# Hybrid attention + PEER layer: group A's keys projected ahead of the transposes of group B's queries, and two pieces of GpSimd work given to VectorE

## The chip, the cores and the metric

One core of a Trainium2 chip runs the whole program. The metric is the device time of one execution in microseconds (us). Engines are named as the profile names them: PE (TensorE, matmuls and transposes), DVE (VectorE), ACT (ScalarE), POOL (GpSimd), SP (SyncE, which issues every transfer here).

## The reference

One decoder layer on 256 tokens of width 1024, in float32. The input is normalised and projected once; the projection is split into group A (sparse attention with compressed, selected and window branches, 8 heads, 2 key/value heads) and group B (latent attention, 8 heads with 96 channels per query and key). Both are mixed by one output projection, and a product-key expert layer (PEER) follows. What the change touches:

```python
proj = rmsnorm(x, norm1_gain) @ w_in                 # q, kc, vc, ks, vs, kw, vw, gate (A), cq, ckv, kr (B)
# group B
q = (rmsnorm(c_q) @ w_uq).reshape(B, S, 8, 96);  kv = (rmsnorm(c_kv) @ w_ukv)
k = concat([k_nope, broadcast(k_rope)]);  q, k = rmsnorm(q, q_gain), rmsnorm(k, k_gain)
q, k = rope(q), rope(k);  p = softmax(q @ k.T * scale, causal);  o_b = p @ v
# group A: k_slc, k_win = rope(rmsnorm(proj columns)); three softmaxes, gated sum -> o_a
h = x + concat([rmsnorm(o_a), rmsnorm(o_b)]) @ w_out
return h + peer_ffn(rmsnorm(h))                      # q projection, top-k, 2 x 128 expert matrices
```

## The kernel before

Tokens stand in two tiles of 128 (`tt` 0 and 1). Every float32 operand of a large product is kept as a rounded part ("hi") and the remainder ("lo"), and a product is three passes: hi·hi, lo·hi, hi·lo. ACT writes the hi part (`split_pack`, L278 for half a pack, L271 for a quarter), DVE or POOL the lo part (DVE at L282, 128x1024; POOL at L273, 128x512).

The input weights come as seven packs, `win[0]` to `win[6]`. Packs 3 and 4 hold group A's queries, pack 5 its keys (ks, kw), pack 6 its values (vs, vw). `mm_pack` (L315) multiplies one token tile by one pack: 24 matmuls. `aq` takes packs 3 and 4, `ak[tt]` takes pack 5 in its first 256 columns and pack 6 in its last 256.

Group B: `b_proj(tt)` multiplies the latents, squares and sums them (L448, L455), takes the power −1/2 on POOL (`rsqrt`: DVE L149, then POOL L150, called the pow below), scales keys `kn` (L458, L459) and queries `qn` (L462), multiplies by the norm weights (keys L460, queries L464) and rotates the queries (L337 to L340). `b_qkT(tt)` (L473) transposes `kn` and `qn`, 8 transposes each, and ACT copies the result (L474). `unit_B` is one group of heads: scores `sB` (L630, L631), row maximum on DVE (L634), exponentials on ACT (L638), scaling on DVE (L640, L642), transposes `pTB` (L648), a copy on ACT (L601), the product with the values `oB` (L656). `finish` (L608 to L618) normalises a group's output and writes its hi and lo parts (`mix`: ACT L610, DVE L611). `a_norm(tt, ...)` (L485 to L494) normalises and rotates group A's queries (8 heads) and later its keys (4 heads); `a_qT` (L506) and `a_kT` (L518) transpose them. `hidden` (L543) and `compress_out` make the compressed keys. `wo_mm` (L999) is the output projection, `unit_A` (L674 to L709) group A's heads.

Up to the line that takes `bp` apart, all engines run in the order of the code. In the stretch that follows, PE and SP are in the order of the code, and DVE, ACT and POOL are put in order by the tile scheduler. From `side = Side(7)` on until `norm2(1)`, SP alone is fixed; PE, DVE, ACT and POOL are in the scheduler's order, which follows the order of the code as a priority and its own estimates of when an instruction is ready. So a line that moves in the code can move many rows on four engines. `beside(gen, n)` emits one pass of a product and then `n` steps of the waiting units (`side`); `do(gen)` emits all of a generator.

```python
        with tc.manual_schedule(engines={mybir.EngineType.SP, mybir.EngineType.PE}):
            next(bp[0])
        ...
        with tc.manual_schedule(engines={mybir.EngineType.SP}):
            side = Side(7)
```

From `split(2)` (L1126) on, all engines are again in the order of the code: the PEER query projection, then 128 expert matrices `u` and 128 `v`.

Of the kernel before, what the change touches and what calls it, by code (L numbers as in the profile page):

```python
# [15 lines left out]
ALU = mybir.AluOpType  # L16
# [69 lines left out]
def body(tc, nc, ap, dbg=None):  # L86
    V, A, T, G, S = nc.vector, nc.scalar, nc.tensor, nc.gpsimd, nc.sync
# [6 lines left out]
    with ExitStack() as ctx:  # L94
# [30 lines left out]
        def bank(name, tag="ps"):  # L125
            return ps.tile([128, 512], F32, tag=tag, name=name, bufs=4 if tag == "ps" else 2)
# [11 lines left out]
        def small(shape, name, dt=F32, bufs=None):  # L138
            return sm.tile(shape, dt, tag=name, name=name, bufs=bufs or 2)
# [6 lines left out]
        def rsqrt(out, ss, n, p=128, m=1):  # L146

            x = small([128, 16], "rs_x")[:p, :m]
            V.tensor_scalar(x, ss, 1.0 / n, EPS, op0=ALU.mult, op1=ALU.add)  # L149
            G.tensor_tensor(out, x, mhalf[:p, :m], op=ALU.pow)  # L150
# [32 lines left out]
        gKC, gBQ, gBK = gB[:, 0:64], gB[:, 64:160], gB[:, 160:256]  # L183
# [16 lines left out]
        kn = scrB[:, 1536:2304].rearrange("p (h d) -> p h d", h=8)  # L200
# [109 lines left out]
        def mm_pack(o, tt, w, xT=xnT):  # L310

            hi, lo = w
            for n, (q, ww) in enumerate(((0, hi), (1, hi), (0, lo))):
                for k in range(8):
                    T.matmul(o, lhsT=xT[:, k, q, tsls[tt]], rhs=ww[:, k, :], start=(n == 0 and k == 0), stop=(n == 2 and k == 7))  # L315
                yield
# [5 lines left out]
        def do(gen):  # L322
            for _ in gen:
                pass
# [107 lines left out]
        def b_proj(tt, tag):  # L432

            tsl = tsls[tt]
            ssq = small([128, 16], "b_ss")
            rb = small([128, 16], "b_rs")
            bk = bank("bk")
            T.matmul(bk, lhsT=ckvT[:, tsl], rhs=wukv[:, 0:512], start=True, stop=True)
            sqk = r_sq()
            A.activation(out=sqk, in_=bk, func=AF.Square)  # L440
            bq = []
            for i in range(2):
                b = bank("bq%d" % i, tag)
                bq.append(b)
                for k in range(2):
                    T.matmul(b[:, :384], lhsT=cqT[:, k, tsl], rhs=wuq[:, k, i * 384:(i + 1) * 384], start=(k == 0), stop=(k == 1))
                A.activation(out=sqb[:, i * 384:(i + 1) * 384], in_=b[:, :384], func=AF.Square)
            V.tensor_reduce(out=ssq[:, 8:16], in_=sqk.rearrange("p (h d) -> p h d", h=8), axis=AX.X, op=ALU.add)  # L448
            V.tensor_scalar(ssq[:, 8:16], ssq[:, 8:16], krss[:, tt:tt + 1], None, op0=ALU.add)
            rsqrt(rb[:, 8:16], ssq[:, 8:16], 96.0, 128, 8)  # L450
            yield
            bvv = bank("bv")
            T.matmul(bvv, lhsT=ckvT[:, tsl], rhs=wukv[:, 512:1024], start=True, stop=True)
            A.activation(out=vB[:, tt, :], in_=bvv, func=AF.Copy)
            V.tensor_reduce(out=ssq[:, 0:8], in_=sqb.rearrange("p (h d) -> p h d", h=8), axis=AX.X, op=ALU.add)  # L455
            rsqrt(rb[:, 0:8], ssq[:, 0:8], 96.0, 128, 8)
            yield
            V.tensor_tensor(kn[:, :, 0:64], bk.rearrange("p (h d) -> p h d", h=8), rb[:, 8:16, None].broadcast_to((128, 8, 64)), op=ALU.mult)  # L458
            V.tensor_tensor(kn[:, :, 64:96], rkr[:, tt, None, :].broadcast_to((128, 8, 32)), rb[:, 8:16, None].broadcast_to((128, 8, 32)), op=ALU.mult)  # L459
            G.tensor_tensor(kn[:, :, 0:64], kn[:, :, 0:64], gBK[:, None, 0:64].broadcast_to((128, 8, 64)), op=ALU.mult)  # L460
            for i in range(2):
                V.tensor_tensor(qn[:, i * 4:(i + 1) * 4, :], bq[i][:, :384].rearrange("p (h d) -> p h d", h=4),  # L462
                                rb[:, i * 4:(i + 1) * 4, None].broadcast_to((128, 4, 96)), op=ALU.mult)
            V.tensor_tensor(qn, qn, gBQ[:, None, :].broadcast_to((128, 8, 96)), op=ALU.mult)  # L464
            rotate(qn[:, :, 64:96], 8, 16, tt, 1)
            yield

        def b_qkT(tt):
            for src, dst in ((kn, kTb), (qn, qTb)):
                for i in range(2):  # L470
                    bt = bank("bT")
                    for h in range(4):
                        T.transpose(bt[:96, h * 128:(h + 1) * 128], src[:, i * 4 + h, :], ident)  # L473
                    A.activation(out=dst[:96, i * 4:(i + 1) * 4, tsls[tt]], in_=bt[:96, :].rearrange("p (h t) -> p h t", h=4), func=AF.Copy)  # L474
                    yield
# [317 lines left out]
        with tc.manual_schedule():  # L793
# [5 lines left out]
            win = {}  # L799

            def load_win(gi):
                win[gi] = load_pack(ap["win"][:, offs[gi]:offs[gi + 1]], WIN_GROUPS[gi], "win", 2 if gi else 4)
# [4 lines left out]
            def split_win(gi, q, e, what="hl"):  # L807
                win[gi][1](q, e, what)
# [77 lines left out]
        with tc.manual_schedule():  # L886
# [14 lines left out]
            def aqm(tt, h):  # L901
                if tt not in aq:
                    aq[tt] = accum("aq")
                do(mm_pack(aq[tt][:, h * 256:h * 256 + 256], tt, win[3 + h][0]))
# [47 lines left out]
# [4 lines that stand above are left out]
            aqm(1, 0)  # L956
            split_win(4, 1, V)
            next(bl)
            aqm(0, 1)
            next(bp[1])  # L960
            do(bl)
            load_win(5)
            next(bp[1])
            open_win(5)
            split_win(5, 0, V)
            split_win(5, 1, V)
            qkT0()
            next(bp[1])
            load_win(6)
            aqm(1, 1)  # L970
            open_win(6)
            split_win(6, 0, V)
            load_w1()
            split_win(6, 1, G)
            an = [a_norm(tt, aq[tt], 0, 8) for tt in range(2)]

        with tc.manual_schedule(engines={mybir.EngineType.SP}):
# [45 lines left out]
            def beside(gen, n):  # L1023

                for _ in gen:
                    side.step(n)
                    ticks[0] += 1
                    while extra and extra[0][0] <= ticks[0]:
                        extra.pop(0)[1]()
# [3 lines left out]
            ak = [bank("ak", "lg"), bank("ak", "lg")]  # L1033
            side.add(*ub[:2])
            side.step(3)
            do(b_qkT(1))
            side.add(*ub[2:])
            beside(mm_pack(ak[0][:, 0:256], 0, win[5][0]), 2)
            do(an[0])
            beside(mm_pack(ak[1][:, 0:256], 1, win[5][0]), 0)  # L1040
            do(an[1])
            mixT = slot(3, "mix", F32R).rearrange("p (c s t) -> p c s t", c=8, s=2)
            aS = slot(4, "aS", F32R)
# [532 lines left out]
```

## Time and profile before

| what | value |
|---|---|
| time, median of 3 runs (lowest to highest) | 967.76 us (965.28 to 968.68) |
| the profiled execution: its own time | 968.06 us |
| its span, first to last instruction | 966.3 us |
| busy: PE, PE's weight loads, DVE, ACT, POOL | 938.3, 848.8, 723.9, 499.2, 180.2 us |
[...]

The span is 1.8 us shorter than the time of its execution, which has a little before the first and after the last instruction. Busy time is summed over stages that have different limits. A time like 64.97 below is counted from the start of the span. Where an instruction's row has brackets at its end, the engine stood idle that long before it, and the name behind the arrow is what ended the idle time.

### The profile page before, as it was taken

The page shows a single profiled execution, that of the slowest core. Times are in us where ns is not written, and L with a number is a line of the kernel's source. Part 1 is how long each engine was busy: PE and PEld are TensorE (multiplying, and loading weights), DVE is VectorE, ACT ScalarE, POOL GpSimd, SP SyncE. Part 2 cuts the span into 40 slices and gives each one's busy share as a digit, 9 for nine tenths or more (in the row PEclk, how much of TensorE's full clock was granted, in tenths as well). Part 3 has the DMA queues.
Part 4 walks back from the last instruction along what each step waited for, and adds up shares of the span by engine and source line. Part 5 has one row for each costly group of instructions (what it writes and reads, how often), then busy time and mean ns, then how long its engine had stood idle before and what let it go on. Part 6 is the DMA issues. An engine that isn't in the chain of part 4 may idle for free.

```text
span 966.3 us, 17204 instructions
## 1 busy us (share of the span) xinstructions
PE 938.3 (97%) x6657; PEld 848.8 (88%) x6657; DVE 723.9 (75%) x1405; ACT 499.2 (52%) x921; POOL 180.2 (19%) x145
## 2 busy tenths in 40 slices
PE   7969999999899999999999999999999999999998
PEld 6857679999899999999999999988888888888886
DVE  6877988767989978889999995566666666666664
ACT  4645756655455464554444544555554444555552
POOL 4443424367028300000111112100000000000000
PEclk9999999999999999999999999999999999999999
DMA  9433322554476575555545555665656666656564
GB/s 329 163 94 115 127 66 88 179 171 136 156 214 197 182 213 171 153 159 163 160 154 154 164 161 179 190 196 188 192 195 195 195 196 195 195 191 192 190 195 150
DMA packets 47314, 166.74 MB, mean 173 GB/s; under 512 B 5504, under 2 KB 6528, under 8 KB 46976
## 3 DMA queue, kind: packets, MB, share of 16 engines
q1 hardware_dynamic: 47232, 165.64, 53.9%
q8 instruction: 52, 0.85, 0.4%
q14 instruction: 30, 0.25, 0.1%
HBM read 163.52 MB, written 2.10 MB: 171 GB/s over the span
## 4 chain that ended last, share of the span: by engine, by line
PE 87%; DVE 7%; ACT 2%; POOL 2%; issue 1%; DMA 1%; SPq 0%; DVEq 0%; POOLq 0%
PE y L1493 36%; PE a L1120 35%; PE q L1120 4%; PE g L1336 3%; PE wo L999 1%; PE ak L315 1%; PE low L315 1%; PE s L1429 1%; DMA B<-keys 1%; PE oA L709 1%; PE pTA L698 1%; POOL lo L784 0%; DVE rq L1402 0%; PE sA L675 0%; DVE win L282 0%
## 5 line engine op out<-in xcount | busy, mean ns | idle before, releaser
L784 DVE TENSOR_TENSOR lo<-raw,hi 128x1024 fp32r<-128x1024 f32 x236 | 289.2, 1228 | 97.3 <-ACT hi L781 95.1
L781 ACT ACTIVATE hi<-raw 128x1024 fp32r<-128x1024 f32 x266 | 279.9, 1053 | 43.7 <-DMA raw<-u 36.9
L1493 PE MATMUL y<-hi,w 128*128 128x512 f32 x1024 | 274.6, 389 | 0.0
L1120 PE MATMUL a<-xtT,hi 128*128 128x256 f32 x2048 | 265.7, 283 | 0.0
L1120 PEld LDWEIGHTS a<-xtT,hi 128*128 128x128 f32 x2048 | 248.0, 190 | 0.4 <-issue 0.4
L1493 PEld LDWEIGHTS y<-hi,w 128*128 128x128 f32 x1024 | 192.0, 188 | 40.2 <-ACT w L1223 0.3
L1493 PE MATMUL y<-lo,w 128*128 128x512 f32 x512 | 158.3, 389 | 0.0
L1120 PE MATMUL a<-xtT,lo 128*128 128x256 f32 x1024 | 140.0, 279 | 3.8 <-DVE lo L784 3.8
L1223 ACT ACTIVATE w<-B 128x256 fp32r<-128x256 f32 x128 | 53.5, 418 | 171.2 <-PE y L1493 171.1
L1120 PEld LDWEIGHTS a<-xtT,lo 128*128 128x128 f32 x1024 | 128.4, 189 | 4.0 <-DVE lo L784 4.0
L1493 PEld LDWEIGHTS y<-lo,w 128*128 128x128 f32 x512 | 96.1, 188 | 19.9
L1224 DVE TENSOR_TENSOR w<-B,w 128x256 fp32r<-128x256 f32 x128 | 54.4, 426 | 70.1 <-ACT w L1223 70.1
L784 POOL TENSOR_TENSOR lo<-raw,hi 128x1024 fp32r<-128x1024 f32 x30 | 72.3, 2420 | 52.2 <-ACT hi L781 51.9
L1468 POOL TENSOR_TENSOR B<-gl,B 128x512 f32<-128x512 f32 (+33 forms) x37 | 29.9, 808 | 257.6 <-ACT gl L1467 257.6
L1351 ACT ACTIVATE B<-g 128x64 f32<-128x64 f32 (+29 forms) x121 | 23.7, 245 | 76.7 <-DVE B L1349 76.7
L1461 ACT ACTIVATE B<-a 128x512 f32<-128x512 f32 (+33 forms) x59 | 28.1, 476 | 61.8 <-PE a L1120 61.6
L1324 DVE TENSOR_TENSOR oh<-misc,con 128x1024 f16<-128x1024 f16 x64 | 57.2, 894 | 0.0
L1328 DVE TENSOR_TENSOR oh<-oh,gf 128x1024 f16<-128x1024 f16 x64 | 44.3, 692 | 2.2
L1349 DVE TENSOR_TENSOR B<-g,B 128x8 f32<-128x8 f32 (+32 forms) x69 | 32.8, 481 | 10.0 <-ACT B L1461 9.8
L1336 PE MATMUL g<-oh 128*128 128x128 f16 x512 | 39.7, 220 | 0.0
L1120 PE MATMUL q<-xrT,hi 128*128 128x256 f32 x256 | 35.4, 284 | 0.0
L1120 PEld LDWEIGHTS q<-xrT,hi 128*128 128x128 f32 x256 | 31.9, 189 | 0.1
(316 smaller groups left out, 897.2 us busy)
## 6 DMA issues: line engine op xcount, KB each, us to landing
raw<-u SPq DMA_DIRECT2D x128, 512.0 KB, 3.6
raw<-v SPq DMA_DIRECT2D x128, 512.0 KB, 4.1
raw<-wq SPq DMA_DIRECT2D x16, 512.0 KB, 3.7
win<-win SPq DMA_DIRECT2D x10, 512.0 KB, 7.5
w<-w SPq DMA_DIRECT2D x8, 512.0 KB, 4.6
wo<-wout SPq DMA_DIRECT2D x8, 512.0 KB, 6.0
wsm<-wu SPq DMA_DIRECT2D x1, 1280.0 KB, 9.1
xx<-x SPq DMA_DIRECT2D x4, 256.0 KB, 3.5
```

The costliest lines, as they stand in the source:

```text
L781: A.activation(out=hi, in_=src, func=AF.Copy)
L784: e.tensor_tensor(lo, src, hi.bitcast(F32), op=ALU.subtract)
L1120: T.matmul(out, lhsT=w[:, k, :], rhs=xT[:, k, q, :], start=(n == 0 and k == 0), stop=(n == 2 and k == 7))
L1223: A.activation(out=w[:, 0, :], in_=b, func=AF.Copy)
L1224: V.tensor_tensor(w[:, 1, :], b, w[:, 0, :].bitcast(F32), op=ALU.subtract)
L1324: V.tensor_tensor(o[:, 0:2].rearrange("p a t (i two) -> p (a t) i two", two=2), iot.rearrange("p (i two) -> p i two", two=2)[:, None].broa ...
L1328: V.tensor_tensor(pairs(o[:, 2:4]), pairs(o[:, 1:2]).broadcast_to((128, 2, 4, 64, 2)), gf[:, t4, :, :, None, :].broadcast_to((128, 2, 4, 6 ...
L1336: T.matmul(b[:, i, :], lhsT=o[:, 0, i, :], rhs=o[:, 2 + q, i, :], start=(q == 0), stop=(q == 1))
L1349: V.tensor_tensor(w, bv[:, c0:m, :], w, op=ALU.mult)
L1461: A.activation(out=dst[:, :, td:], in_=bv[:, :, td:], func=AF.Gelu_apprx_tanh)
L1468: (G if j < 127 else V).tensor_tensor(dst[:, :, :td], a[:, :, :td], dst[:, :, :td], op=ALU.mult)
L1493: T.matmul(ya[tt][n], lhsT=wh[:, q, tt * 128:(tt + 1) * 128], rhs=src[:, n * 512:(n + 1) * 512], start=(jj == 0 and p == 0), stop=(jj == 1 ...
```

## The change

The norm weights of group B's keys (L460) and the lo part of the second half of pack 6 (written at L273 by POOL before, at L282 by DVE after) go from POOL to DVE. In the code of the scheduled stretch, the product of pack 5 with token tile 0 now stands ahead of the transposes `b_qkT(1)`, and the number of steps of the units taken beside the two products of pack 5 changes from 2 and 0 to 1 and 2.

```diff
-            G.tensor_tensor(kn[:, :, 0:64], kn[:, :, 0:64], gBK[:, None, 0:64].broadcast_to((128, 8, 64)), op=ALU.mult)
+            V.tensor_tensor(kn[:, :, 0:64], kn[:, :, 0:64], gBK[:, None, 0:64].broadcast_to((128, 8, 64)), op=ALU.mult)
...
-            split_win(6, 1, G)
+            split_win(6, 1, V)
...
             side.step(3)
+            beside(mm_pack(ak[0][:, 0:256], 0, win[5][0]), 1)
             do(b_qkT(1))
             side.add(*ub[2:])
-            beside(mm_pack(ak[0][:, 0:256], 0, win[5][0]), 2)
             do(an[0])
-            beside(mm_pack(ak[1][:, 0:256], 1, win[5][0]), 0)
+            beside(mm_pack(ak[1][:, 0:256], 1, win[5][0]), 2)
             do(an[1])
```

What the scheduler makes of it is seen at three places.

**PE, from the second block of scores on.** Before, right behind the scores of token tile 0 (`win_587` is pack 5, `win_655` pack 6):

```order
L631 MATMUL sB<-cm 128x512
L473 MATMUL bT<-con,scrB 96x128 x8
L315 MATMUL ak<-win_587,xnT 128x256 x2
L473 MATMUL bT<-con,scrB 96x128 x8
L315 MATMUL ak<-win_587,xnT 128x256 x24
L630 MATMUL sB<-qkB 128x256 x2
L631 LDWEIGHTS cm
L631 MATMUL sB<-cm 128x2x128
L648 MATMUL pTB<-con,wsm 128x128 x4
L315 MATMUL ak<-win_587,xnT 128x256 x22
```

After:

```order
L631 MATMUL sB<-cm 128x512
L315 MATMUL ak<-win_587,xnT 128x256 x48
L315 MATMUL ak<-win_655,xnT 128x256
L648 MATMUL pTB<-con,wsm 128x128
L473 MATMUL bT<-con,scrB 96x128
L648 MATMUL pTB<-con,wsm 128x128
L473 MATMUL bT<-con,scrB 96x128
L648 MATMUL pTB<-con,wsm 128x128 x2
L473 MATMUL bT<-con,scrB 96x128 x14
L656 MATMUL oB<-PT,vB 64x128 x4
L648 MATMUL pTB<-con,wsm 128x128 x4
```

All 48 matmuls of pack 5 now stand ahead of the 16 transposes of token tile 1, and the first transposes of probabilities stand ahead of those too.

**DVE, up to the first scaling of probabilities (L642).** `scrB` holds `kn`, `qn` and group A's queries; `a_ss` and `a_rs` are group A's sums and their powers. Before:

```order
L634 TENSOR_REDUCE nmB<-sB 128x4 x2
L337 TENSOR_TENSOR fe<-scrB,cm 128x128
L338 TENSOR_TENSOR fe<-scrB,cm 128x8x8
L339 TENSOR_TENSOR fe<-scrB,cm 128x8x8
L486 TENSOR_REDUCE a_ss<-fe 128x8
L340 TENSOR_TENSOR scrB<-fe 128x8x16
L149 TENSOR_SCALAR rs_x<-a_ss 128x8
L490 TENSOR_SCALAR a_rs<-a_rs,misc 128x8
L492 TENSOR_TENSOR scrB<-aq,a_rs 128x512
L640 RECIPROCAL suB<-suB 128x4
L493 TENSOR_TENSOR scrB<-scrB,wsm 128x512
L642 TENSOR_SCALAR wsm<-wsm,suB 128x128 x4
```

After:

```order
L282 TENSOR_TENSOR win_655<-win,win_655 128x1024
L634 TENSOR_REDUCE nmB<-sB 128x4 x2
L490 TENSOR_SCALAR a_rs<-a_rs,misc 128x8
L486 TENSOR_REDUCE a_ss<-fe 128x8
L492 TENSOR_TENSOR scrB<-aq,a_rs 128x512
L149 TENSOR_SCALAR rs_x<-a_ss 128x8
L493 TENSOR_TENSOR scrB<-scrB,wsm 128x512
L490 TENSOR_SCALAR a_rs<-a_rs,misc 128x8
L337 TENSOR_TENSOR fe<-scrB,cm 128x128
L640 RECIPROCAL suB<-suB 128x4
L338 TENSOR_TENSOR fe<-scrB,cm 128x8x8
L642 TENSOR_SCALAR wsm<-wsm,suB 128x128 x4
```

The second L490, which needs a pow from POOL, still stands ahead of L642, now with L493 between it and the L149 that feeds the pow; the rest of token tile 1's queries of group A (L492, L493) has moved behind L642.

**PE, around the last product of group B with its values.** `wo_1306` and `wo_1317` are the output projection of token tile 0, `wo_1341` and `wo_1351` that of tile 1, which reads what `finish` makes of this last `oB`. Before:

```order
L656 MATMUL oB_683<-PT_93,vB_92 64x128 x4
L674 MATMUL sA_1152<-aS_838 128x512
L675 MATMUL sA_1152<-aS_838 128x512
L677 LDWEIGHTS cm_89
L677 MATMUL sA_1152<-cm_89 128x2x128
L999 MATMUL wo_1306<-wo0_1101,mix_837 128x256 x7
L999 MATMUL wo_1341<-wo0_1101,mix_837 128x256 x4
L717 LDWEIGHTS cm_89
L717 MATMUL oA_1099<-cm_89 128x512
L999 MATMUL wo_1341<-wo0_1101,mix_837 128x256 x8
```

After:

```order
L677 MATMUL sA_1138<-cm_89 128x2x128
L999 MATMUL wo_1317<-wo0_1104,mix_848 128x256 x4
L656 MATMUL oB_682<-PT_93,vB_92 64x128 x4
L999 MATMUL wo_1351<-wo0_1104,mix_848 128x256 x4
L999 MATMUL wo_1394<-wo0_1104,mix_848 128x256
L717 LDWEIGHTS cm_89
L717 MATMUL oA_1102<-cm_89 128x512
L999 MATMUL wo_1394<-wo0_1104,mix_848 128x256
L999 MATMUL wo_1351<-wo0_1104,mix_848 128x256 x6
```

The block of scores and the seven matmuls that stood between the last `oB` and its reader are no longer there.

## Rows read from the trace of the kernel before

**Rows 1.** The page, chain of work that ended last: shares of the span by engine.
```profile
PE 87%; DVE 7%; ACT 2%; POOL 2%; issue 1%; DMA 1%; SPq 0%; DVEq 0%; POOLq 0%
```

**Rows 2.** Timeline of PE: start, duration (us), engine, line, operation, tiles, count, [idle before].
```profile
52.93 3.12 PE L315 MATMUL aq<-win,xnT 128*128 128x256 f32 x24
...
58.11 1.03 PE L473 MATMUL bT<-con,scrB 128*96 128x128 f32 x8
...
64.97 1.91 PE L473 MATMUL bT<-con,scrB 128*96 128x128 f32 x8 [5.46 <-DVE scrB L340]
...
70.20 1.03 PE L630 MATMUL sB<-qkB 96*128 96x256 f32 x4
...
72.28 0.83 PE L648 MATMUL pTB<-con,wsm 128*128 128x128 f32 x4 [0.94 <-DVE wsm L642]
...
85.70 1.04 PE L506 MATMUL aT<-con,scrB 128*128 128x128 f32 x8
...
101.09 0.28 PE L677 MATMUL sA<-cm 128*128 128x256 bf16 x1
```

**Rows 3.** Windows: stretch, length, busy us and count by engine, PEclk, DMA, GB/s.
```profile
65.00:68.00 3.00, 3.00 (x15) 2.93 (x16) 3.00 (x7) 1.41 (x9) 0.00 (x0) 0.50 0.32 76
...
72.30:85.70 13.40, 13.40 (x108) 12.21 (x109) 8.45 (x33) 4.99 (x16) 1.01 (x1) 1.00 0.00 1
...
97.00:111.00 14.00, 11.91 (x88) 8.86 (x85) 13.48 (x32) 9.58 (x26) 10.04 (x9) 1.00 0.56 179
```

**Rows 4.** Timeline of DVE, columns as in rows 2.
```profile
52.03 0.67 DVE L486 TENSOR_REDUCE a_ss<-fe 128x8 f32<-128x512 f32 x1
...
54.53 0.69 DVE L458 TENSOR_TENSOR scrB<-bk,b_rs 128x512 f32<-128x512 f32 x1 [0.89 <-POOL b_rs L150]
...
58.40 1.02 DVE L462 TENSOR_TENSOR scrB<-bq,b_rs 128x384 f32<-128x384 f32 x2 [1.60 <-POOL b_rs L150]
60.00 1.22 DVE L490 TENSOR_SCALAR a_rs<-a_rs,misc 128x8 f32<-128x8 f32 x1 [0.58 <-POOL a_rs L150]
...
64.75 1.21 DVE L282 TENSOR_TENSOR win<-win,win 128x1024 fp32r<-128x1024 f32 x1
...
70.26 0.23 DVE L490 TENSOR_SCALAR a_rs<-a_rs,misc 128x8 f32<-128x8 f32 x1 [1.75 <-POOL a_rs L150]
...
71.25 0.69 DVE L493 TENSOR_TENSOR scrB<-scrB,wsm 128x512 f32<-128x512 f32 x1
71.86 0.87 DVE L642 TENSOR_SCALAR wsm<-wsm,suB 128x128 f32<-128x128 f32 x4
...
104.60 0.68 DVE L611 TENSOR_TENSOR mix<-fe,mix 128x512 fp32r<-128x512 f32 x1
...
106.60 1.27 DVE L690 TENSOR_TENSOR suA<-suA,misc 128x2 f32<-128x2 f32 x1
```

**Rows 5.** Timeline of POOL, columns as in rows 2.
```profile
40.43 2.67 POOL L150 TENSOR_TENSOR b_rs<-rs_x,mhalf 128x8 f32<-128x8 f32 x1 [0.36 <-DVE rs_x L149]
...
55.30 1.47 POOL L460 TENSOR_TENSOR scrB<-scrB,wsm 128x512 f32<-128x512 f32 x1 [0.80 <-DVE rs_x L149]
56.73 1.63 POOL L150 TENSOR_TENSOR b_rs<-rs_x,mhalf 128x8 f32<-128x8 f32 x1
...
59.94 3.27 POOL L273 TENSOR_TENSOR win<-win,win 128x512 fp32r<-128x512 f32 x2
```

**Rows 6.** Waits of PE from 85 to 163 us: total, times, longest.
```profile
PE aT L518 <- DVE scrB L340: 1.3, 1, 1.3
PE cmp L573 <- DVE cm L568: 1.1, 1, 1.1
PE wo L999 <- DVE mix L611: 0.6, 1, 0.6
```

**Rows 7.** Windows around PE's other long wait, columns as in rows 3.
```profile
247.00:251.10 4.10, 0.29 (x3) 0.09 (x1) 3.89 (x17) 0.77 (x2) 0.00 (x0) 1.00 0.00 0
...
252.50:255.50 3.00, 3.00 (x16) 3.00 (x15) 2.93 (x6) 0.96 (x1) 0.00 (x0) 0.50 0.42 156
```

## The prediction

> **What bounds the kernel now.** I read the chain of work that ended last first: 87% of it is PE [rows 1], so a time is won where PE waits, and a microsecond of DVE or POOL counts only if PE is behind it. Then PE's timeline. Its longest wait is 5.46 us, from 59.51 to 64.97, ahead of the second eight transposes `bT`, and DVE's L340, the end of the query rotation, ends it [rows 2]. A second, 0.94 us, follows at 72.28 ahead of the first `pTB`, ended by DVE's L642 [rows 2]. From there to 85.70 PE is busy 13.40 of 13.40 us [rows 3]: PE-bound. So what the first half of this stretch really delivers is the moment 72.28: whatever PE gained before it, it would still have waited for L642. The next weak place is 97 to 111 us, where DVE is busy 13.48 of 14.00 us and PE 11.91 [rows 3].
>
> [...]
>
> **The change, part by part.**
>
> *When L642 is ready.* The sum goes along DVE's order. Three steps.
>
> First, L462 of token tile 1 starts at 58.40 because it waits for a pow on POOL [rows 4]. That pow could have begun at 55.30 but stood behind L460, until 56.73 [rows 5]: moving L460 off POOL gives 1.4 us. Ahead of this, L486 (0.67 us) and one L282 (1.21 us) now stand behind the L149 that feeds the other pow [rows 4]; that L149 comes about 1.7 us earlier, and the L282 is put right behind it, in the time that DVE idled before L458 (0.89 us [rows 4]) and a little more. L458 then starts at about 52.9 in place of 54.53: 1.6 us. L460 on DVE costs about L493's 0.69 us (same shape [rows 4]); both copies lie inside DVE's waits for a pow and cost nothing, and without those waits 1.4 us. So L462 starts at 58.40 − 1.4 − 1.6 = 55.4; with the pow starting only when DVE's L459 ends (see below), 55.7.
>
> Second, from L462 to L642 it was 71.86 − 58.40 = 13.46 us [rows 4]. Out of it go: the idle 0.58 ahead of L490 and 0.99 of that L490 (1.22 against 0.23 when POOL is not running L273 [rows 4, 5]); L492 and L493 of token tile 1, two of 0.69, and some 0.3 of small rotations, which now stand behind L642. Into it come L486 (0.67) and the second L282 of pack 6 (1.21), which POOL did in 3.27 us [rows 5]. Net −0.58 − 0.99 − 1.38 − 0.3 + 0.67 + 1.21 = −1.4.
>
> Third, the second L490 still waits for its pow. Before it idled 1.75 us [rows 4]. Now L493 stands in that time. If POOL runs beside it, the idle time left is 1.1 us; if POOL has to wait for L493 first, 1.7. What the row shows: one pow took 2.67 us, against 1.63, while DVE ran an L282 of pack 4 [rows 5], so POOL was held until that ended. I take the held case for most of it: −0.2.
>
> [...]
>
> So L642 starts at 55.7 + 13.46 − 1.6 = 67.6, less up to 0.5 since L337 too ran beside L273: 67.1. `pTB` starts 72.28 − 71.86 = 0.42 later: 67.5 in place of 72.28, between 67.0 and 68.0.
>
> *What PE has to do from there to `aT` (85.70).* Before, 13.42 us. To add: 16 transposes `bT`, at 1.03 for eight less overlap, 1.8; one score block that was already done, 1.03 and its mask, 1.1 [rows 2]; one small sum of `finish`, 0.3. To take off: 49 instead of 26 matmuls of `ak` are already done, 23 at 3.12/24 = 0.13 [rows 2], less overlap 2.8. That is 13.8 us, and `aT` starts at 81.3: **−4.4 us**.
>
> *The clock.* PE now runs out of work at 63.4 (the 24 `aq` from about 52.0, the two score blocks, 49 `ak`) and idles 4.1 us. Idle times of 5.46 us and of 3.8 us (4.10 less 0.29 busy) were followed by half clock [rows 2, 3, 7]; after the 0.94 us at 72.28 the clock stayed full [rows 2, 3]. 4.1 is nearest to 3.8, so I take a fall. Both falls fill a window of 3.0 us [rows 3, 7]; with their edges I count up to 3.5, of which half is lost on whatever work lies in it: from nothing, if it lies in the idle time, to 1.75 us. This time PE does not wait afterwards. I take **+1.4 us**, near the upper end, as in both rows the half clock lies on work.
>
> [...]
>
> *From `aT` on.* Three waits can go: 1.3 us for group A's keys, 1.1 for the compressed keys [rows 6], since `finish` of token tile 0, four DVE instructions of which L611 is one, now stands among DVE's waits before 81 us and no longer among these. One wait grows. The output projection of tile 1 needs `mix` of the last `oB`. Before, L611 ended at 105.28, 3.9 us after the preceding score block's end at 101.37 [rows 2, 4], and the block of scores and seven matmuls filled the time; the wait was 0.6 [rows 6]. Now PE has four matmuls and the `oB`, 1.1 us, then four, 0.5, and DVE has five instructions more and one less ahead of L611, taken as 0.7 in all (one L493): 3.9 + 0.7 − 1.6 = 3.0 us of waiting, 2.4 more. Bounds: all three waits gone and none grown, −3.0; none gone and one grown, +2.4. Two gone and one grown is 0, and what DVE sheds with `finish` covers a part: I take **−0.6 us**. All later stages are in the order of the code behind a busy PE, and move as they are.
>
> *Elsewhere.* No transfer is added or moved; SP's order is the same. Pack 6's raw buffer is free at about 61.5 rather than 63.2, which helps the last `w1` transfer and nothing waits for it.
>
> **Sum:** −4.4 + 1.4 − 0.6 = −3.6 us on the profiled execution's 968.06: 964.5 us. That execution lies 0.3 us above the median of the runs shown, so the change against the median is −3.3 us, 0.34%. What a measurement of this kernel can tell from no change is about 0.3%, 2.9 us: faster means below 964.9, slower above 970.7.
>
> **The rivals.**
>
> *More is won.* The clock does not fall, or in the idle time, and the waits of rows 6 mostly go: −4.4 − 2.0 = −6.4, 961.7 us. For it: the fall is worth nothing if it lies before 67.5. Against it: the new wait for `mix`.
>
> *The wait is only moved.* PE's 5.46 us becomes 4.1 us at `pTB`, the fall is paid in full, and DVE, nearly full from 97 to 111 us, gives none back: −4.4 + 1.75 + 1.2 = −1.5, 966.6 us. For it: PE still idles 4.1 us, and DVE's load in that stretch [rows 3].
>
> *Slower.* One mechanism: in the stretch around the last `oB` POOL's lo parts of the output weights hold DVE's short instructions ahead of L611. L690 took 1.27 us there where the small L490 takes 0.23, 1.0 us lost [rows 4]. With nothing left on PE to cover it, each such hold ahead of L611 is 1.0 us of waiting. Seven of them turn −3.6 into +3.4, 971.5 us, and it decides from six. Against it: half of the dozen rows ahead of L611 would have to be held, and POOL ran 10.04 of those 14 us before as well [rows 3].
>
> *The change doesn't do what it says:* POOL's L460 and L273 hide anyway and the scheduler's new order is as good as the old, 968. Against it: the pow at 56.73 does wait for L460 [rows 5].
>
> **How the numbers follow.** Forecast (963 to 966) 0.50; the wait only moved 0.24; more won 0.14; slower 0.08; nothing 0.04. Of the forecast some two thirds lie below 964.9, so faster is 0.34 + 0.14 = 0.48; slower 0.08; the rest, 0.44, is within 0.3%. The range takes in the bounds of the costs: −4.9 + 0 − 2.0 = −6.9 below and −3.9 + 1.75 + 1.5 = −0.6 above, 961.2 to 967.5; that leaves out less than 2 in 10. The forecast's own range is 963 to 966.
>
> **What would show it.** In the profile after: L462 of tile 1 at 55.4 to 56.0; POOL without L460; one wait of PE of 3.5 to 4.5 us ahead of `pTB` L648 in place of the one ahead of L473; the pow ahead of the second L490 held by L493; `aT` at 81 to 83.2; half clock for some 3.5 us near 64 to 72; a wait of 2 us or more of L999 for `mix`; L518's 1.3 gone. The prediction is wrong if `pTB` starts later than 69 (DVE's order costs more than its rows), or if PE's waits from 81 to 108 us sum to over 5 us.

## The result

The change made the kernel slower: 973.30 us (median of 6 runs, 970.63 to 975.12) against 968.63 us of the kernel before on the same chip (6 runs, 965.28 to 970.22), a ratio of 1.0054 with a 95% interval of 1.0034 to 1.0074. I had forecast 964.5. The profiled execution of after took 971.82 us, its span is 970.0 us, and TensorE's mean granted clock is 0.989 (0.996 before).

**The first half did what was forecast.** PE's timeline after (start, duration, engine, line, operation, tiles, count, [idle before]), to be read against [rows 2]:

```profile
68.70 0.42 PE L648 MATMUL pTB<-con,wsm 128*128 128x128 f32 x1 [4.91 <-DVE wsm L642]
...
83.74 1.04 PE L506 MATMUL aT<-con,scrB 128*128 128x128 f32 x8
```

In place of 5.46 us ahead of `bT` PE waits 4.91 us ahead of `pTB`, and `aT` starts at 83.74 in place of 85.70 [rows 2]. This execution had lost 0.8 us already before the change (the first `bT` starts at 50.56, before at 49.75), so the gain by `aT` is nearer 2.8 us.

**The loss lies between `aT` and the query projection of the expert layer.** The first matmul of that projection, L1120, stands behind the same work in both kernels. Its row says when the first and the last of the line's matmuls ran; first the kernel before, then after:

```profile
L1120 PE MATMUL q<-xrT,hi x256: 276/281/384, 162.4 to 215.1; 128*128 128x256 f32 x128
```

```profile
L1120 PE MATMUL q<-xrT,hi x256: 276/276/388, 168.1 to 219.1; 128*128 128x256 f32 x128
```

From `aT` to the first `q` it was 162.4 − 85.7 = 76.7 us before and is 168.1 − 83.7 = 84.4 us after: 7.7 us more, where I had forecast 0.6 less. From the first `q` to the end it was 803.9 us before and is 801.9 in this execution, so nothing behind it adds to the loss. The waits of PE after, over the whole run (us in total, times, longest), against [rows 6]:

```profile
PE pTB L648 <- DVE wsm L642: 4.9, 1, 4.9
...
PE wo L999 <- ACT mix L610: 3.5, 1, 3.5
PE aT L518 <- DVE scrB L340: 1.6, 1, 1.6
PE wo L999 <- DVE mix L611: 1.2, 1, 1.2
PE pTA L698 <- DVE wsm L692: 1.0, 2, 0.7
```

The wait for `mix` has grown from 0.6 to two, 3.52 us for the hi part (L610) and 1.25 us for the lo part (L611); the wait ahead of L518 has not gone (1.3, now 1.6); the one for the compressed keys (1.1) has. PE's timeline and DVE's around it:

```profile
101.02 0.66 PE L656 MATMUL oB<-PT,vB 128*64 128x128 f32 x8
105.19 0.85 PE L999 MATMUL wo<-wo,mix 128*128 128x256 f32 x5 [3.52 <-ACT mix L610]
...
107.64 1.65 PE L999 MATMUL wo<-wo,mix 128*128 128x256 f32 x6 [1.25 <-DVE mix L611]
```

```profile
100.66 0.69 DVE L680 TENSOR_REDUCE nmA<-sA 128x2 f32<-128x512 f32 x1 [1.80 <-PE sA L677]
101.27 1.18 DVE L561 TENSOR_SCALAR fe<-fe 128x256 f32<-128x256 f32 x1
102.37 0.47 DVE L1003 SCALAR_TENSOR_TENSOR xx<-wo,misc,xx 128x256 f32<-128x256 f32 x1
102.77 1.11 DVE L562 TENSOR_TENSOR fe<-fe,cm 128x256 f32<-128x256 f32 x1
103.80 0.68 DVE L608 TENSOR_TENSOR fe<-oB,pp 128x512 f32<-128x512 f32 x1
104.40 0.77 DVE L563 TENSOR_SCALAR fe<-fe 128x256 f32<-128x256 f32 x1
...
105.27 1.07 DVE L690 TENSOR_TENSOR suA<-suA,misc 128x2 f32<-128x2 f32 x1
106.38 0.62 DVE L692 TENSOR_SCALAR wsm<-wsm,suA 128x256 f32<-128x256 f32 x2
106.91 0.68 DVE L611 TENSOR_TENSOR mix<-fe,mix 128x512 fp32r<-128x512 f32 x1
```

The last `oB` ends at 101.68 and its reader on DVE, L608, starts at 103.80, behind L680, L561, L1003 and L562; L611 is ready to be read only at 107.6. Before, L608 stood ahead of L561 and L562 and started right behind the end of its `oB` at 101.97:

```profile
102.14 0.69 DVE L608 TENSOR_TENSOR fe<-oB,pp 128x512 f32<-128x512 f32 x1
102.75 0.49 DVE L561 TENSOR_SCALAR fe<-fe 128x256 f32<-128x256 f32 x1
...
103.76 0.92 DVE L562 TENSOR_TENSOR fe<-fe,cm 128x256 f32<-128x256 f32 x1
```

So the scheduler's new order is one on two engines: VectorE puts other rows ahead of L608. And PE has nothing to do meanwhile: the score block and seven matmuls that stood there before are elsewhere. POOL runs L273 throughout:

```profile
87.60 5.28 POOL L512 TENSOR_TENSOR aS<-xx,aS 64x512 fp32r<-64x512 f32 x4 [1.16 <-ACT aS L499]
...
98.37 7.95 POOL L273 TENSOR_TENSOR wo<-wo,wo 128x512 fp32r<-128x512 f32 x6 [0.32 <-ACT wo L271]
```

Last, the granted clock. Before, it fell once up to 163 us (at 65 to 68, [rows 3]). After, windows (stretch, length, busy us and count of PE, PEld, DVE, ACT, POOL, then PEclk, which is the granted clock with 1 for full speed, DMA, GB/s):

```profile
68.00:72.00 4.00, 3.30 (x16) 3.22 (x17) 4.00 (x19) 1.57 (x3) 0.00 (x0) 0.59 0.00 0
92.00:96.00 4.00, 4.00 (x38) 1.97 (x40) 3.04 (x9) 3.56 (x10) 1.38 (x2) 0.58 0.64 218
...
104.00:108.00 4.00, 1.56 (x8) 1.21 (x9) 3.93 (x9) 1.42 (x3) 2.32 (x2) 0.79 0.19 36
108.00:112.00 4.00, 4.00 (x13) 2.53 (x12) 2.77 (x6) 0.00 (x0) 0.56 (x1) 0.50 0.26 104
112.00:116.00 4.00, 4.00 (x16) 2.94 (x16) 2.09 (x6) 1.81 (x6) 0.00 (x0) 0.50 0.00 0
116.00:120.00 4.00, 4.00 (x29) 3.27 (x29) 2.20 (x9) 2.71 (x13) 0.55 (x1) 0.93 0.00 0
```

There are three falls to half clock (0.50). The first is the one that I had forecast. The second follows the wait ahead of L518, the third the first wait for `mix`. In that one PE is busy in all of the 8 us from 108 to 116 and still runs at half clock: 29 matmuls in 8 us where the four us behind them hold 29.

### The profile page after: what moved, and what is told of

Same layout as the page of the kernel before. It is cut to its first block, busy times and chain, and to the rows that moved or that the text cites. A ratio compares the mean times of both kernels' runs of the same rounds, so it can differ in the third digit from the quotient of the medians.

```text
span 970.0 us, 17202 instructions
## 1 busy us (share of the span) xinstructions
PE 942.7 (97%) x6657; PEld 851.4 (88%) x6657; DVE 721.8 (74%) x1408; ACT 499.5 (51%) x921; POOL 176.0 (18%) x141
## 4 chain that ended last, share of the span: by engine, by line
PE 88%; DVE 7%; POOL 2%; issue 1%; ACT 1%; DMA 0%; SPq 0%; DVEq 0%; POOLq 0%; ACTq 0%
PE y L1493 36%; PE a L1120 35%; PE q L1120 5%; PE g L1336 3%; PE wo L999 2%; PE low L315 1%; PE s L1429 1%; DVE win L282 1%; PE pTA L698 1%; PE sA L675 1%; PE oA L709 1%; POOL b_rs L150 1%; POOL lo L784 0%; DVE rq L1402 0%; PE sA L674 0%
## 5 line engine op out<-in xcount | busy, mean ns | idle before, releaser
L1120 PE MATMUL a<-xtT,hi 128*128 128x256 f32 x2048 | 264.8, 282 | 0.0
L1120 PEld LDWEIGHTS a<-xtT,hi 128*128 128x128 f32 x2048 | 247.3, 189 | 0.4 <-issue 0.4
L1120 PE MATMUL a<-xtT,lo 128*128 128x256 f32 x1024 | 140.2, 280 | 4.1 <-DVE lo L784 4.1
L1120 PEld LDWEIGHTS a<-xtT,lo 128*128 128x128 f32 x1024 | 128.3, 189 | 4.5 <-DVE lo L784 4.5
L1351 ACT ACTIVATE B<-g 128x64 f32<-128x64 f32 (+29 forms) x121 | 23.6, 244 | 76.7 <-DVE B L1349 76.7
L999 PE MATMUL wo<-wo,mix 128*128 128x256 f32 x192 | 32.5, 309 | 4.8 <-ACT mix L610 3.5
L1120 PE MATMUL q<-xrT,hi 128*128 128x256 f32 x256 | 34.7, 281 | 0.0
```

The costliest lines, as they stand in the source:

```text
L999: T.matmul(o, lhsT=mixT[:, ab * 4 + c, q, tsls[tt]], rhs=ww[:, (n % 2) * 4 + c, :], start=(m == 0 and c == 0), stop=(m == 2 and c == 3))
L1120: T.matmul(out, lhsT=w[:, k, :], rhs=xT[:, k, q, :], start=(n == 0 and k == 0), stop=(n == 2 and k == 7))
```

## The experiments

Three theories of the 7.7 us. **Theory 1, order:** the moved line and the step counts made the scheduler put the first reader of tile 1's `mix` right behind its producer, with nothing between. **Theory 2, engines:** L460 and pack 6 on VectorE load it, so that L611 comes late. **Theory 3, holds:** POOL's L273 holds DVE's rows ahead of L611, that is, they take longer while it runs. To this comes the question what the half clock costs of it. Every ratio is against the kernel before, run on the same chip beside it; the last three columns are of the one profiled execution.

| kernel | median us | before, us | ratio (95%) | `aT` | first `q` | between |
|---|---|---|---|---|---|---|
| before | | | | 85.70 | 162.4 | 76.7 |
| after | 973.30 | 968.63 | 1.0054 (1.0034 to 1.0074) | 83.74 | 168.1 | 84.4 |
| e1_engines | 960.67 | 967.58 | 0.9925 (0.9905 to 0.9945) | 81.42 | 158.2 | 76.8 |
| e2_order | 974.51 | 967.58 | 1.0063 (1.0043 to 1.0083) | 88.33 | 170.4 | 82.1 |
| d24_fill | 977.44 | 967.58 | 1.0108 (1.0081 to 1.0134) | 82.66 | 168.6 | 85.9 |
| p_lo | 967.51 | 967.58 | 0.9987 (0.9972 to 1.0003) | 82.86 | 161.9 | 79.0 |
| e1a_L460 | 964.69 | 969.66 | 0.9960 (0.9941 to 0.9979) | 81.82 | 158.5 | 76.7 |
| e1b_pack6 | 968.24 | 969.66 | 0.9985 (0.9965 to 1.0005) | 83.84 | 160.6 | 76.8 |
| d20_fill | 971.75 | 969.66 | 1.0016 (0.9996 to 1.0037) | 83.21 | 166.0 | 82.8 |
| s02_counts | 963.54 | 969.66 | 0.9953 (0.9934 to 0.9972) | 81.32 | 158.1 | 76.8 |
| w_after | 968.73 | 967.40 | 1.0008 (0.9985 to 1.0031) | 82.62 | 165.0 | 82.4 |
| s11_counts | 966.95 | 967.40 | 0.9996 (0.9974 to 1.0018) | 82.74 | 164.1 | 81.4 |
| e1_again | 964.07 | 967.40 | 0.9950 (0.9928 to 0.9972) | 80.27 | 157.0 | 76.7 |
| e1_loop | 963.17 | 967.40 | 0.9948 (0.9925 to 0.9971) | 79.91 | 156.6 | 76.7 |

The last column is the one to read first: it does not depend on what an execution lost or won before `aT`.

### The two engine moves alone, and the order alone

`e1_engines` is the kernel before with these two lines of the change:

```diff
-            G.tensor_tensor(kn[:, :, 0:64], kn[:, :, 0:64], gBK...
+            V.tensor_tensor(kn[:, :, 0:64], kn[:, :, 0:64], gBK...
...
-            split_win(6, 1, G)
+            split_win(6, 1, V)
```

> The kernel before with only the two engine moves: L460 and the lo parts L273 of pack 6 on VectorE; the step counts and the place of the first keys' pack stay as before. Theory 1 (the loss is made by the new order on PE between aT and the compressed keys: in the changed kernel only four matmuls of the output projection stand between the last oB and the first that reads mix of token tile 1, before it was a whole score block and seven): this kernel keeps the order of before in that stretch, so no wait for mix over 1.0 us (before 0.6), no half clock from aT to cmp, aT to cmp within 1 us of the 24.6 us of before; the time is 966 to 969. Theory 2 (the two engine moves load VectorE and that delays L611): the wait for mix is 2 us or more in this kernel too, and the time is 971 to 974.

`e2_order` is the changed kernel with these two lines put back, so that the moved line and the step counts are left.

> The changed kernel with L460 and the lo parts of pack 6 put back on GpSimd; the first keys' pack stays ahead and the step counts are the new ones. Theory 1 (order): PE's order from aT on is that of the changed kernel, so the wait for mix stays at 2.5 us or more (3.5 there), followed by half clock, and the time is 972 to 975. Theory 2 (engine moves): the wait for mix goes below 1.5 us and the time is 967 to 970.

Theory 2 falls as the cause, in both directions. With the engine moves alone the stretch from `aT` takes what it took before, the wait for `mix` is 0.6 us, the clock is full (1.00) in the windows of 68 to 72, 92 to 96 and 100 to 120 us, and the kernel is faster than I had expected of either theory. With the order alone PE waits 3.1 us for `mix`, half clock follows from 108 to 118 (0.50 in the windows from 108 to 116, 0.77 from 116 to 120), and the kernel is slower than before. In the new order the moves do add something: `aT` to `q` is 84.4 us with them and 82.1 without, with 4.8 against 3.4 us of waiting for `mix` and 1.6 against 0.3 ahead of L518. These are one execution each, and no run separates what makes the difference. `e2_order` is slower early on too: without the moves, L642 is so late for the new order that PE waits 8.1 us ahead of `pTB`. The waits of `e2_order` from 45 to 170 us:

```profile
PE pTB L648 <- DVE wsm L642: 8.9, 3, 8.1
PE wo L999 <- ACT mix L610: 3.1, 1, 3.1
```

### GpSimd's lo parts taken out of the stretch

```diff
-            beside(split_wo(1), 1)
+            r1, half1 = split_pack(wos[1], wo_slot[1], 256, "wo1")
+            wos[1] = ((r1[0], r1[0]), half1)
+            for q in range(4):
+                half1.part(q, G, "h")
+                side.step(1)
```

> The changed kernel without GpSimd's four lo parts (L273) of the second pack of output weights; the projection reads the hi parts in their place, so this part of the result is left out. The order on every other engine is unchanged. Theory 3 (GpSimd's L273 holds VectorE's short instructions ahead of L611): L561, L562, L563 and L690, which took 1.18, 1.11, 0.77 and 1.07 us in the changed kernel, fall to the 0.49, 0.92, 0.28 and 0.23 of rows where GpSimd is not running, 2.2 us in all; the wait for mix goes from 3.5 to about 1.3 us; if that is what sets off the half clock too, the time falls by 4 us or more, to 967 to 970. Theory 1 (order alone): L611 hardly moves, the wait stays at 3 us or more, and the time stays at 972 to 975.

Theory 3 holds, and for more than I had given it: I had taken the 0.49 and 0.92 us of L561 and L562 in the kernel before as undisturbed, but POOL ran L273 there too, from 98.06 to 104.39. DVE's timeline of `p_lo`, the same rows in the same order as in the fence of after above, and POOL's, which now ends at 99.8:

```profile
99.80 0.69 DVE L680 TENSOR_REDUCE nmA<-sA 128x2 f32<-128x512 f32 x1 [0.97 <-PE sA L677]
100.41 0.28 DVE L561 TENSOR_SCALAR fe<-fe 128x256 f32<-128x256 f32 x1
100.61 0.48 DVE L1003 SCALAR_TENSOR_TENSOR xx<-wo,misc,xx 128x256 f32<-128x256 f32 x1
101.00 0.41 DVE L562 TENSOR_TENSOR fe<-fe,cm 128x256 f32<-128x256 f32 x1
101.33 0.68 DVE L608 TENSOR_TENSOR fe<-oB,pp 128x512 f32<-128x512 f32 x1
101.93 0.28 DVE L563 TENSOR_SCALAR fe<-fe 128x256 f32<-128x256 f32 x1
...
102.33 0.16 DVE L690 TENSOR_TENSOR suA<-suA,misc 128x2 f32<-128x2 f32 x1
...
103.05 0.69 DVE L611 TENSOR_TENSOR mix<-fe,mix 128x512 fp32r<-128x512 f32 x1
```

```profile
94.64 5.13 POOL L273 TENSOR_TENSOR wo<-wo,wo 128x512 fp32r<-128x512 f32 x4 [2.63 <-issue]
```

From L680's start to L611's it is 3.25 us where after has 6.25. The four rows L561, L562, L563 and L690 give 0.90, 0.70, 0.49 and 0.91 us, 3.00 in all: the whole difference. The first two stand ahead of L608 and give back 1.60 us, as much as the wait for the hi part loses (3.52 to 1.9); the other two stand ahead of L611, and the wait for the lo part goes. The rows that read PSUM (L680, L1003, L608) are as long in both kernels (0.69, 0.47 and 0.68 us after; 0.69, 0.48 and 0.68 in `p_lo`). Some 3.4 us of half clock are left between 100 and 108 (0.83 in the window to 104, 0.74 in the one to 108), and the first `q` starts 6.2 us earlier. The stretch from `aT` falls from 84.4 to 79.0 us, so 5.4 of the 7.7 us are gone and 2.3 are left. Why L273 holds those four rows and not these three, no run shows.

### Something for TensorE to do in the wait

```diff
                 hi, lo = wos[(1 - ab) * 2 + n // 2][0]
+                if (tt, n, ab) == (1, 0, 1):
+                    for i in range(24):
+                        T.matmul(o, lhsT=mixT[:, 4 + i % 4, 0, tsls[0]], rhs=hi[:, i % 4, :], start=True, stop=True)
```

> The changed kernel with 24 more matmuls of the shape of the output projection put right ahead of the first one that reads mix of token tile 1; they read token tile 0's mix, which is there, and what they write is overwritten. They take 24 x 0.13 = 3.1 us, which is less than the wait of 3.5 us they stand in, and work nothing out that is needed. [...] Theory 1b (the waits themselves are the loss, the clock is not): nothing is won, 972 to 975.

This one could not be read for its time, which lies above the range of theory 1b and so above that of theory 1a, by which most of the loss is the half clock behind the wait. In its profile, of the fastest of its six executions, the clock stayed full from 100 to 120 (1.00 in each window of 4 us), as theory 1a has it, but the wait for `mix` kept 1.7 us, and the scheduler put the rows behind it in another order, which brought a wait of 2.71 us at 127.84 and slower matmuls behind that (fourteen of L709 took 1.97 us at 130.62 where they took 1.09 at 121.10). So I ran the same with `range(20)`, which leaves the order up to the compressed keys alone:

> As the kernel with 24 matmuls in the wait for mix of token tile 1, with 20: 20 x 0.13 = 2.6 us, and here PE's order up to the compressed keys stays that of the changed kernel, which it did not with 24 (there the clock stayed full from 106 to 117 and aT to cmp fell from 32.1 to 28.4 us, but the rows behind it stood in another order and gave more back). Theory 1a (the half clock behind the wait costs some 3 to 4 us): clock 1.00 from 106 to 117, aT to cmp 28 to 29 us, time 968 to 971. Theory 1b (the waits alone are the loss): aT to cmp stays above 31 us, time 972 to 975.

PE's timeline of `d20_fill` (L1002 there is L999; L999 there is the filler), and its windows:

```profile
101.14 2.65 PE L999 MATMUL wo<-wo,mix 128*128 128x256 f32 x20
104.76 0.74 PE L1002 MATMUL wo<-wo,mix 128*128 128x256 f32 x4 [0.97 <-ACT mix L610]
...
107.21 0.98 PE L1002 MATMUL wo<-wo,mix 128*128 128x256 f32 x6 [1.36 <-DVE mix L611]
```

```profile
108.00:112.00 4.00, 4.00 (x16) 2.61 (x15) 3.21 (x5) 0.18 (x1) 0.56 (x1) 0.62 0.20 83
112.00:116.00 4.00, 4.00 (x28) 3.01 (x28) 2.10 (x7) 3.34 (x15) 0.55 (x1) 0.96 0.00 0
```

With 2.65 us of the wait filled by matmuls that nobody needs, tile 1's projection starts as late behind `aT` as after (21.55 against 21.45 us), yet from `aT` to `q` it takes 1.6 us less: the half clock behind the waits lasts some 3.4 us in place of 10. PE's busy time in the stretch, without the filler, is 74.7 against 77.0 us after, so 6.8 us less of half clock in it are worth some 2.3. That is half of what theory 1a expected (30.2 us from `aT` to the compressed keys lies between its range and theory 1b's): a second wait, 1.36 us, stood behind the filler and the clock fell there. The ratio of 1.0016 against 1.0054 agrees, with intervals that overlap a little.

The next kernel fills the wait with work that is needed, by the order of the projection's loop:

```diff
-            for n in range(4):
-                for tt in range(2):
+            for n, tt in ((0, 0), (1, 0), (0, 1), (1, 1), (2, 0), (2, 1), (3, 0), (3, 1)):
                     beside(wo_mm(tt, n, 1), 2)
```

> The changed kernel with the loop of the output projection in another order: the second column block of token tile 0 before the first of tile 1, so that 12 matmuls that need nothing of tile 1's mix stand behind the last oB in place of 4; no work is added. Theory 1 (the reader stands too close behind its producer): 8 more x 0.13 = 1.05 us of cover, the wait of 3.5 us for mix falls to 2.3 to 2.6 us, the second one of 1.25 goes (the second column block of tile 1 no longer stands in it), half clock behind it is shorter, aT to cmp falls from 32.1 to 29 to 31 us, time 0.2 to 0.4% below the changed kernel. Theory 3 (only GpSimd's holds count): as these rows do not move on VectorE, nothing is won, 972 to 975.

The waits fall to 1.92 and 0.59 us, and the ratio to 1.0008, whose interval ends just below the one of after. PE's timeline of `w_after`:

```profile
100.57 1.69 PE L999 MATMUL wo<-wo,mix 128*128 128x256 f32 x12
104.17 0.86 PE L999 MATMUL wo<-wo,mix 128*128 128x256 f32 x5 [1.92 <-ACT mix L610]
105.96 1.44 PE L999 MATMUL wo<-wo,mix 128*128 128x256 f32 x5 [0.59 <-DVE mix L611]
```

Behind the last `oB` now stand twelve matmuls, 1.69 us, where after has none (four stand ahead of it in both), so the eight of my estimate were too few. The reader starts as late behind `aT` as after (21.55 us), and the first wait is shorter by these twelve: 1.60 us. The second is shorter as L611 starts 0.6 us earlier behind `aT`, with L692 now behind it. So theory 3's "nothing is won" falls as a complete account. One part of theory 1 fails: the half clock is no shorter, 10.2 us from 105 to 115 (0.63, 0.50 and 0.59 in the windows from 104 to 116). From `aT` to `q` only 2.0 of the 7.7 us are back, no more than the shorter waits give.

### Other step counts

`s02_counts`:

```diff
-            beside(mm_pack(ak[0][:, 0:256], 0, win[5][0]), 1)
+            beside(mm_pack(ak[0][:, 0:256], 0, win[5][0]), 0)
...
-            beside(mm_pack(ak[1][:, 0:256], 1, win[5][0]), 2)
+            beside(mm_pack(ak[1][:, 0:256], 1, win[5][0]), 1)
```

> The changed kernel with other step counts: the first keys' pack is still put ahead of group B's query transposes and both engine moves stay, but the pack ahead lets the score blocks step 0 times and the other pack 1 time, in place of 1 and 2. In the order of PE the transposes bT then stand between the two packs of ak again, and from aT to the compressed keys the rows are those of before (two score blocks around the last oB, seven matmuls of the output projection behind them). Theory 1 (the loss is this order, which the step counts set, not the place of the pack as such): the wait for mix is 1 us or less, no half clock from 90 to 125, aT to cmp within 1 us of 24.6 us, time 960 to 964. Rival (the keys' pack ahead is the loss wherever the rest stands): 970 to 974.

Theory 1, as expected: the keys' pack still stands ahead of `b_qkT(1)`, and yet the stretch from `aT` takes 76.8 us, with a wait of 0.6 for `mix` and full clock (1.00) in the windows of 92 to 96 and 100 to 120. So the place of the pack is not the loss; what the counts made of the later order is. DVE's L608 stands ahead of L561 and L562 there, as before, and so it does in the kernels with the engine moves alone; no run has the old order on one of the two engines and the new one on the other, so their shares are not known. That `w_after`, with 1.69 us of cover on PE, still waits says only that PE's side is not the whole.

`s11_counts` has 1 and 1 in these two lines. In it token tile 0's sum of squares of group B's output is taken from a buffer that the keys' norm has reused (L485 writes it at 82.01, L617 reads at 84.27), so tile 0's scale is another number.

> The changed kernel with step counts 1 and 1 in place of 1 and 2. Up to the first pTB PE's order is that of the changed kernel, so PE's wait ahead of pTB stays at 4.5 to 5 us with half clock behind it; around the last oB stand the end of a score block and five matmuls ahead of the first that reads mix of tile 1, 1.3 us in place of 0.6. Theory 1 (the order around the last oB sets the loss): the wait for mix is 1 to 2.5 us, aT to cmp 26 to 30 us, and the time lies between the kernel before and the changed one, 966 to 971. Rival (the half clock and the 4.9 us wait ahead of pTB are the loss): it stays at 972 to 975, as these are the same.

PE's wait ahead of `pTB` is 4.9 us as after, with half clock in the whole window from 68 to 72 (0.50), longer than after's 3.4 us; the wait for `mix` is 2.1 us and half clock behind it ends at 110.5 (0.50 in the window from 104 to 108, 0.68 in the next). The time, 966.95, is that of the kernel before: again theory 1, and the early wait and its half clock are not what made the change slower.

### Which engine move pays, and what the best kernel is worth

The two moves apart, each from the kernel before: `e1a_L460` with the first pair of lines of the diff of `e1_engines`, `e1b_pack6` with the second.

> The kernel before with L460 alone moved to VectorE (the lo parts of pack 6 stay on GpSimd). By my prediction's first step the pow ahead of L462 of token tile 1 then starts at once, some 1.4 us earlier, and the query rotation L340 that ends PE's 5.46 us wait comes as much earlier; the order of PE from there on is that of before. Theory of the sum (each move frees its own part of PE's wait): 966 to 967.2, against 967.6 of before and 960.7 with both moves. Rival (the 6.9 us of both moves come from L460 alone, since both rows stand behind one another on GpSimd): 960 to 963.

> The kernel before with the lo parts of pack 6 alone moved to VectorE (L460 stays on GpSimd). Theory of the sum: GpSimd's 3.27 us of L273 at 59.94 no longer hold L490 (1.22 us for 0.23) and L337, and the scheduler puts VectorE's rows ahead of L340 in another order; L340 comes 1.5 to 3 us earlier, 963 to 966. Rival (both moves act through L460 alone): no change, 967 to 968.5.

L460 alone shortens PE's wait ahead of `bT` from 5.46 to 2.9 us (with one of 2.6 now ahead of `pTB`) and gives 0.40%; pack 6 alone shortens it to 4.0 us and gives 0.15% (its interval reaches 1.0005). Both ratios add up, within their intervals, to what both give together, as the theory of the sum has it, but with the larger share on L460, where I had put the smaller one.

`e1_again` is `e1_engines` run once more, `e1_loop` is `e1_engines` with the loop of `w_after`.

> The kernel with only the two engine moves once more, for its interval and for a second profile: its first profiled execution, 967.0, lay 6 us above its median of 960.67 though the first q projection began 4.2 us earlier than before. If the moves are worth what the trace shows up to that projection: ratio 0.994 to 0.997. If the first median is right: 0.991 to 0.994.

> The kernel with only the two engine moves, and the output projection's loop in the order with the second column block of tile 0 ahead of the first of tile 1. In the kernel with the two engine moves the wait for mix is 0.6 us; 8 more matmuls of cover take it away: 0.6 us at most, 0 to 0.1% below that kernel, which its measurement hardly tells from nothing. If it is slower, the second block's earlier place costs somewhere else.

The two engine moves alone were faster than before by 0.75% and 0.50% in two sets of runs. The trace supports the smaller: the first `q` starts 4.2 and 5.4 us earlier. PE's timeline of `e1_again` shows the wait ahead of `bT` that is left and, around `mix`, the old pattern:

```profile
60.77 1.05 PE L473 MATMUL bT<-con,scrB 128*96 128x128 f32 x8 [2.92 <-DVE scrB L340]
...
97.34 1.68 PE L999 MATMUL wo<-wo,mix 128*128 128x256 f32 x11
99.88 1.50 PE L999 MATMUL wo<-wo,mix 128*128 128x256 f32 x10 [0.62 <-DVE mix L611]
```

With the loop's other order (`e1_loop`) the wait for `mix` goes and one of 0.78 us for L1003 takes its place; the time is the same. So the version to keep is the change without its moved line and its new step counts; `s02_counts`, with the moved line and other counts, cannot be told from it (0.9953).

## Why the prediction was wrong

**What held.** The pow ahead of the second L490 was held (2.06 us beside L493, where one at 45.14 took 1.64); one wait stands ahead of `pTB` in place of that ahead of `bT`, though 4.91 us is above the 3.5 to 4.5 of the forecast; `pTB` starts at 68.70, under the 69 that I had set; half clock follows from 68.8 to 72.2. Two misses cancel on the way, which is luck. L462 of token tile 1 starts at 56.99, 0.5 us behind the forecast of 55.7 even with the 0.8 us lost ahead of it: the L282 that I had counted as free held the pow ahead of L458 (2.54 against 1.64 us). From L462 to L642 it took 11.3 us in place of the 11.9 of my sum. My "−4.4 + 1.4" puts `aT` 3.0 us earlier, at 82.7; after has 83.74, and four experiments with the same order up to there (`d24_fill`, `p_lo`, `d20_fill`, `w_after`) have 82.6 to 83.2.

**The step that failed** is the term "From `aT` on", −0.6 us, which measured +7.7. It put holds of VectorE's rows and a fall of the clock behind the wait for `mix` at nothing. (The range was too narrow even by its own bounds: this term's −3.0 to +2.4 stood in it as −2.0 to +1.5.) Its parts:

- *The wait for `mix`*, put at 3.0 us, is 4.77 in two pieces. I had counted 0.7 us for VectorE's extra rows at their undisturbed durations, on top of the 3.9 us from the end of the score block to the end of L611 before. That path is 7.0 us after (100.62 to 107.59), 2.4 more than my 4.6. The holds on L561, L562, L563 and L690 are 3.0 us, as `p_lo` shows, and 0.7 of them (L561 and L562) stood in the 3.9 already.
- *The wait ahead of L518*, which I had let go, stayed. L340 ends it, and the three small rows of that rotation (L337, L339, L340) take 1.22, 1.28 and 1.33 us while POOL runs L512, against 0.2 for the same rows at 84 us before: by that, holds again (no run takes L512 away), not the rows of `finish` that I had moved out.
- *The clock.* I had counted a fall for the wait ahead of `pTB` and none for the wait that I had myself let grow to 3.0 us, while the rows already had a fall behind 3.8 us of idleness [rows 7]. PE's time between `aT` and the first `q`, before and after (columns as in the windows above):

```profile
85.70:162.40 76.70, 72.14 (x581) 55.85 (x579) 66.13 (x185) 52.77 (x159) 32.69 (x30) 1.00 0.32 105
```

```profile
83.74:168.10 84.36, 76.95 (x577) 58.93 (x576) 65.24 (x186) 51.09 (x156) 32.17 (x29) 0.92 0.28 95
```

PE stands idle 4.6 us before and 7.4 after, 2.8 more. The other 4.8 of the 7.7 us are busy time for the same work, and some 13.6 us of it are at half clock, about 0.35 us for each. By the same sum `p_lo` has 1.4 us for 3.4 of half clock, `d20_fill` 2.5 for 6.8 and `w_after` 5.3 for 13.6; `d24_fill` and `s11_counts`, with another order of rows, have nearer 0.6 for each. This split is worked out, not measured by itself.

**The rival that named it.** "Slower" had the right place and mechanism, at a chance of 0.08. Its price was wrong: it needed six holds of 1.0 us, since it counted the wait alone. Four holds of 0.5 to 0.9 us on a wait without cover were there, and the clock went down with it. My own bound for being wrong, waits of PE over 5 us from 81 to 108, was met with 6.3. The other rivals took the waits behind `aT` as growing by 1.2 us at most.

The change has two halves of opposite sign: the engine moves, −0.50 to −0.75% alone, and the moved line with the counts 1 and 2, which costs 1.0 to 1.3% on top of them. Of the loss in the second half, order and holds are both needed: without the order (`e1_engines`, `s02_counts`) GpSimd holds rows too (L690 takes 1.27 us in `e1_engines`), but the wait for `mix` stays at 0.6 us, and without the holds (`p_lo`) 5.4 of the 7.7 us between `aT` and `q` are gone.

## What to carry to other kernels

Where a scheduler places the rows, look at what stands between each late producer and its first reader in the new order and price that wait with VectorE's durations beside a running GpSimd (here up to 0.9 us more for a row of 0.2 to 0.4). Count the clock with every wait that you let grow: here half clock followed waits of 1.4 to 5.5 us, though not every one (in `p_lo` the clock stayed at 1.00 from 92 to 96, behind 1.6 us), lasted 3.4 to 10.2 us and cost some 0.35 us for each (worked out, as above). And try the parts of a change apart: one half of this one made the kernel faster, and the whole made it slower.

## What was not expected of the hardware

- Half clock outlasted its cause: after the first wait for `mix`, TensorE ran at half clock (0.50) for some 10 us, with PE busy 8.00 of 8.00 us from 108 to 116. In the same place it was 3.4 us in `p_lo` and `d20_fill`, but 10.2 in `w_after`, whose first wait (1.92 us) is that of `p_lo` (1.91). So the length of the wait alone does not decide it, and what does is open.
- The same row order and the same wait of 1.6 us ahead of L518 were followed by half clock at 92 to 96 in three profiles (after, at 0.58, `d20_fill`, at 0.59, and `w_after`, at 0.65), and not in two (`d24_fill` and `p_lo`, both at 1.00). So neither the order nor the wait alone decides it, and no run shows what does.
- The matmuls of L1120 spread over 51.0 us after (168.1 to 219.1) and 52.7 us before (162.4 to 215.1), at full clock (1.00); only 0.5 us of the difference is a wait, for the keys' transfer. The median matmul takes 276 ns after and 281 before. It differs between executions of different kernels with the same code there, and I have no cause for it.
